# Gating values by a seven-product scheme, with u computed first

## The chip, the cores and the metric

The kernel runs on one core of a Trainium2 chip. The metric is the device time of one execution in microseconds (us). Five engines work side by side, each with its own instruction queue: TensorE (PE, matmuls), VectorE (DVE), ScalarE (ACT), GpSimd (POOL) and SyncE (SP, which here issues most of the loads). They wait for each other by semaphores.

## The reference, cut to what matters

One layer of a token mixer with 512 tokens of width 1024, and behind it a convolutional feed-forward. What is touched lies in the mixer:

```python
z = h @ w_in                       # (512, 1024) @ (1024, 7200)
u, vs, q, r, ga, gb, k, v, lr = _split(z, IN_SPLITS)
# spatial gating: 4 chunks of 128 tokens, 8 groups of 128 columns
vn = layer_norm(gelu(vs), ln_g, ln_b)
a  = gelu(u) * (einsum('gpq,bnqgc->bnpgc', w_s, vn) + b_s)
# bidirectional gated linear attention (GLA), 4 heads, chunks of 64 tokens
la = log_sigmoid(lr @ w2 + b2) / 16
o  = gla(q, k, v, la)              # products with exp(cumsum(la)), a state from chunk to chunk
ob = o * rsqrt(mean(o * o) + EPS) * g * silu(r)
merged = sigmoid(ga) * (a @ w_br_a) + sigmoid(gb) * (ob @ w_br_b)
return merged @ w_o
```

All of it is float32.

## The kernel before

Each float32 matmul is made of three: both operands are split into a high part (rounded to a short format) and a low part (the rest), and high x high, high x low and low x high are summed in PSUM. A product of 1024 x 1024 weights with all 512 tokens takes 192 matmuls of 128x512 in this way.

The weights come in tiles of 512 KB. A list, `specs`, sets their order. Each time the program asks for the next weights (`weights`), the loads further along in the list are issued on SP (`raw` tiles, five buffers) and the next tiles are split: ScalarE writes the high part `wh` (L152), VectorE the low part `wl` (L153). So the order of the list is also the order of this work on SP, ScalarE and VectorE.

Some products use a scheme of seven block products in place of eight (`w_strassen` L192 for the weights, `strassen` L474 for the matmuls): 7 x 24 = 168 matmuls. The weights' block sums are built partly by accumulating loads that POOL issues into `tt` tiles, partly by VectorE (L233, L245), the activations' sums `s1` to `s4` by `hx_sums` (L1281). Before the change the two output gates GA and GB, R, the output projection and the feed-forward's last matrix use it; the gating values vs, u, and the branches don't.

PSUM has eight banks, two pools of four: `mm` and `gl`. Accumulation, GLA's small products and transposes share them.

The stages around the change, in the program's order: the last GLA heads' work sits in a list `hooks`; `hook()` takes one step of it between groups of matmuls of the running stage. `steps(h)` (L1093) lists a head's steps: transposes, scores, state updates `step_u`, the next head's decays (`step_z`), and the outputs `step_o`. The decays of head 3 are computed on ScalarE as Abs, Exp, Ln for the log-sigmoid (L904, L915, L917 for the tokens, L872, L880, L881, L886 for the context) and Exp of the running sums (L935 to L937). VectorE multiplies the context's keys by the result (L952), and PE transposes the product (L970). Then:

1. vs: 192 matmuls (`wide_tm`), the remaining hooks beside them; Gelu and the statistics of the layer norm;
2. u: 192 matmuls, one block of 128 columns at a time, Gelu on ScalarE; beside it the normalisation of vs in 32 pieces of 128x128 (L1189) and the spatial gating, one group behind each block (`sgu_part`);
3. branch a: `a @ w_br_a`, first the left half in four `mm` banks, then the right half in four `gl` banks (`wide_kk`); beside it `hx_sums`;
4. GA, GB, R by the seven products, then branch b and the rest.

`tick` advances background work for later stages (VectorE's L1211) where it is called. ScalarE computes Exp, Ln, Gelu, Sigmoid and Sqrt from tables; where a function is not in the active table, the program has an instruction `ACT_TABLE_LOAD` ahead of it.

Of the kernel before, what the change touches and what calls it, by code (L numbers as in the profile page):

```python
# [33 lines left out]
def backbone_kernel(  # L34
# [157 lines left out]
    def w_strassen(w, c0, add_b12=False, low_first=False):  # L192
# [24 lines left out]
        def load_t(j):  # L217
            def load():
                tt[j] = [(late if low_first else heap)([P, 512], s="tt") for _ in range(2)]
# [76 lines left out]
    w_strassen(w_o[0], 0, True, True)  # L296
# [720 lines left out]
    def step_u(h, n0, n1):  # L1017
        S_ = heads[h]
        for n in range(n0, n1):
            for d in range(2):  # L1020
                i, j = (n, n + 1) if d == 0 else (3 - n, 2 - n)
                u = gl()
                mm3(u[:, :256], [z[:, i, :] for z in S_["kT"][d]], [z[:, i % 2, :] for z in S_["vx"][i // 2]],
                    True, True)
                raw = heap([P, 256], s="stt")
                V.tensor_tensor(raw, u[:, :256], S_["raw", d], op=ALU.add)
                V.tensor_scalar(raw, raw, S_["dec"][d][:, i:i + 1], None, op0=ALU.mult)
                S_["raw", d] = raw
                split_st(S_["st"][d][j], raw)

    def step_o(h, part):
        S_ = heads[h]
        for i in ((1, 2), (0, 3))[part]:
            po = gl()
# [132 lines left out]
    def vs_done(hf, t, ps):  # L1167
        vraw[hf][t] = late([P, 512], s="vr")
        A.activation(vraw[hf][t], ps, AF.Gelu)
# [16 lines left out]

    def vs_norm(g):
# [46 lines left out]
    crow = [late([110, P], s="crow") for _ in range(2)]  # L1234
    cw = ffn_conv_w[0].rearrange("a b (f p) -> (a b f) p", p=P)
    dma(crow[0], cw[0:110])
    dma(crow[1][0:88, :], cw[110:198])
    dma(crow[1][88:110, :], r8(ffn_conv_b[0]))
    ccol = const([P, 220], "ccol")

    def conv_cols(i):
        ps = gl()
        T.transpose(ps[:, :110], crow[i], ident[:110, :110])
        V.tensor_copy(ccol[:, i * 110:(i + 1) * 110], ps[:, :110])

# [4 lines left out]
    def sgu_part(j, ug):  # L1250
        ps = gl()
        for t in range(4):
            T.matmul(ps[:, t * P:(t + 1) * P], vsn[j][:, t, :], swT[j // 4][:, j % 4, :], start=True, stop=True)  # L1253
        s_ = heap([P, 4, P], s="sg")
        V.scalar_tensor_tensor(s_, ps.rearrange("p (t r) -> p t r", t=4), lng[:, j:j + 1],
                               sgb[j // 4][:, j % 4, :].unsqueeze(1).to_broadcast([P, 4, P]), op0=ALU.mult, op1=ALU.add)
        V.tensor_tensor(ug, s_.rearrange("p t r -> p (t r)"), ug, op=ALU.mult)
        a_act.append(split_act(ug, s="a", eng=A.copy))

    prev = None  # L1260
    vs_norm(0)
    for j in range(KT):
        w = weights()
        ps = mm()
        prod_cm(ps, w, hx)
        ug = heap([P, S], s="ug")
        A.activation(ug, ps, AF.Gelu)
        if prev is not None:
            sgu_part(*prev)
        prev = (j, ug)  # L1270
        if j in (3, 4):
            conv_cols(j - 3)
        if j < KT - 1:
            vs_norm(j + 1)
        tick(2 + j % 2)
    sgu_part(*prev)


    sums = {name: [] for name in ("s1", "s2", "s3", "s4")}

    def hx_sums():  # L1281

        a11, a21, a12, a22 = ([[z[:, c:c + 256] for z in hx[k0 + k]] for k in range(4)]
                              for k0, c in ((0, 0), (0, 256), (4, 0), (4, 256)))
        sums["a11"], sums["a12"], sums["a22"] = a11, a12, a22
        f_ = lambda z: z.bitcast(F32)
        s4_t = None
        for k in range(4):
            u, v = heap([P, 512], s="hu"), heap([P, 512], s="hv")
            s1, q, s3, s4 = u[:, :256], u[:, 256:], v[:, :256], v[:, 256:]  # L1290
            f1, f2 = heap([P, 512], s="hf"), heap([P, 512], s="hf")
            V.tensor_tensor(f1, f_(hx[k][0]), f_(hx[k][1]), op=ALU.add)
            V.tensor_tensor(f2, f_(hx[4 + k][0]), f_(hx[4 + k][1]), op=ALU.add)
            V.tensor_tensor(s1, f2[:, 256:], f1[:, 256:], op=ALU.subtract)
            V.tensor_tensor(s3, f1[:, :256], f1[:, 256:], op=ALU.subtract)  # L1295
            V.tensor_tensor(q, s1, f1[:, :256], op=ALU.add)
            V.tensor_tensor(s4, q, f2[:, :256], op=ALU.subtract)
            yield
            xh, xl = heap([P, 512], F32R, s="xh"), heap([P, 512], F32R, s="xl")
            if k % 2 == 0:  # L1300
                s4_t = heap([P, 512], F32R, s="s4h"), heap([P, 512], F32R, s="s4l")
            o = (k % 2) * 256
            h4, l4 = (z[:, o:o + 256] for z in s4_t)
            h3, l3 = a21[k]
            A.copy(h3, s3)
            V.tensor_tensor(l3, s3, f_(h3), op=ALU.subtract)
            A.copy(xh[:, :256], s1)
            A.mul(xh[:, 256:], q, -1.0)
            V.tensor_tensor(xl[:, :256], s1, f_(xh[:, :256]), op=ALU.subtract)
            V.scalar_tensor_tensor(xl[:, 256:], q, -1.0, f_(xh[:, 256:]), op0=ALU.mult, op1=ALU.subtract)  # L1310
            A.copy(h4, s4)
            V.tensor_tensor(l4, s4, f_(h4), op=ALU.subtract)
            sums["s1"].append((xh[:, :256], xl[:, :256]))
            sums["s2"].append((xh[:, 256:], xl[:, 256:]))
            sums["s3"].append((h3, l3))
            sums["s4"].append((h4, l4))
            yield
# [17 lines left out]

    def br_a_done(hf, t, ps):
        br[t][hf] = late([P, 512], s="br")
        A.copy(br[t][hf], ps)

    summing = hx_sums()  # L1340
    count = [0]

    def br_a_step():
        count[0] += 1
        if count[0] > KT:
            ada_bank[0] = mm
        if count[0] % 2:
            next(summing)
        else:
            tick(3 if count[0] <= KT else 4)  # L1350

    wide_kk(of_cols(a_act), br_a_done, br_a_step)
    a_act.clear()

    def ga_done(hf, t, src, sign):
        sg_ = src if sign < 0 and t > 1 else heap([P, 512], s="sga")
        A.activation(sg_, src, AF.Sigmoid, scale=sign)
        V.tensor_tensor(br[t][hf], br[t][hf], sg_, op=ALU.mult)

    of_sums = lambda name, k, t: [z[:, t * P:(t + 1) * P] for z in sums[name][k]]  # L1360
    ada_bank[0] = gl
    strassen(of_sums, ga_done, lambda: None)
# [32 lines left out]
    count[0] = 0  # L1395
# [562 lines left out]
```

## Time and profile before

| | us |
|---|---|
| median of 3 runs | 916.84 (916.72 to 916.93) |
| the profiled execution | 916.85 |
| its span in the profile | 914.9 |
| PE busy | 897.5 |
| DVE busy | 755.6 |
| ACT busy | 485.0 |
| POOL busy | 62.8 |

The profile is of one execution; times count from the span's start. Its mean granted TensorE clock is 0.996 of full speed. A row of the time line has the start, the time from the first start to the last end of what was merged, the engine, the line, the operation, output and inputs by the program's names, shape and count; in brackets the idle time before it and what ended that. Instructions that follow each other on one engine overlap a little in the records. Wait rows read: engine, line, what it waited for, us in all, times, longest.

### The profile page before, as it was taken

The page shows a single profiled execution, that of the slowest core. Times are in us where ns is not written, and L with a number is a line of the kernel's source. Part 1 is how long each engine was busy: PE and PEld are TensorE (multiplying, and loading weights), DVE is VectorE, ACT ScalarE, POOL GpSimd, SP SyncE. Part 2 cuts the span into 40 slices and gives each one's busy share as a digit, 9 for nine tenths or more (in the row PEclk, how much of TensorE's full clock was granted, in tenths as well). Part 3 has the DMA queues.
Part 4 walks back from the last instruction along what each step waited for, and adds up shares of the span by engine and source line. Part 5 has one row for each costly group of instructions (what it writes and reads, how often), then busy time and mean ns, then how long its engine had stood idle before and what let it go on. Part 6 is the DMA issues. An engine that isn't in the chain of part 4 may idle for free.

```text
span 914.9 us, 12857 instructions
## 1 busy us (share of the span) xinstructions
PE 897.5 (98%) x4671; PEld 755.7 (83%) x4671; DVE 755.6 (83%) x1308; ACT 485.0 (53%) x869; POOL 62.8 (7%) x98
## 2 busy tenths in 40 slices
PE   7999999999999999999999999999999999999996
PEld 5777899998888888888888879988888888888885
DVE  5667786889589878986776897899999888999796
ACT  5156554757366448575652569533333333467573
POOL 3000000000000011122011010000000000123000
PEclk9999999999999999999999999999999999999998
DMA  9960401045089385987586083263444333499522
GB/s 268 332 177 1 139 24 47 1 138 139 9 259 336 93 208 120 295 229 163 160 229 186 21 198 114 84 196 115 131 134 127 104 93 114 104 236 255 129 70 92
DMA packets 125820, 134.26 MB, mean 147 GB/s; under 512 B 7177, under 2 KB 84309, under 8 KB 125757
## 3 DMA queue, kind: packets, MB, share of 16 engines
q1 hardware_dynamic: 115357, 116.80, 41.4%
q0 software_dynamic: 8672, 15.43, 10.1%
q10 hardware_dynamic: 1728, 1.22, 0.4%
q8 instruction: 37, 0.61, 0.3%
q14 instruction: 26, 0.21, 0.1%
HBM read 131.32 MB, written 2.10 MB: 146 GB/s over the span
## 4 chain that ended last, share of the span: by engine, by line
PE 96%; DVE 2%; ACT 1%; DMA 0%; issue 0%; ACTq 0%
PE mm L406 32%; PE mm L437 11%; PE gl L484 9%; PE mm L484 7%; PE gl L1741 6%; PE mm L1741 4%; PE mm L430 4%; PE gl L437 4%; PE gl L956 3%; PE mm L421 3%; PE mm L729 2%; PE gl L729 1%; PE gl L652 1%; PE gl L989 1%; PE gl L1253 1%; PE mm L629 1%
## 5 line engine op out<-in xcount | busy, mean ns | idle before, releaser
L152 ACT CAST wh<-raw 128x1024 fp32r<-128x1024 f32 x110 | 114.7, 1049 | 102.5 <-PE mm L406 71.0
L153 DVE TENSOR_TENSOR wl<-raw,wh 128x1024 fp32r<-128x1024 f32 x110 | 133.4, 1219 | 27.0 <-ACT wh L152 21.8
L1624 DVE SCALAR_TENSOR_TENSOR cacc<-ca,ccol,cacc 128x441 f32<-128x441 f32 (+2 forms) x176 | 120.8, 692 | 6.1 <-ACT cacc L1612 2.8
L406 PE MATMUL mm<-h2h,wh 128*128 128x512 f32 x320 | 124.5, 389 | 0.0
L406 PE MATMUL mm<-h2l,wh 128*128 128x512 f32 x320 | 124.5, 389 | 0.0
L406 PE MATMUL mm<-h2h,wl 128*128 128x512 f32 x320 | 124.5, 389 | 0.0
L406 PEld LDWEIGHTS mm<-h2h,wl 128*128 128x128 f32 x320 | 60.1, 188 | 12.6
L406 PEld LDWEIGHTS mm<-h2l,wh 128*128 128x128 f32 x320 | 60.1, 188 | 12.5
L406 PEld LDWEIGHTS mm<-h2h,wh 128*128 128x128 f32 x320 | 60.1, 188 | 12.3
L1211 DVE SCALAR_TENSOR_TENSOR acc<-wa,c_col,acc 128x512 f32<-128x512 f32 x64 | 45.6, 745 | 4.0 <-DMA wa<-in_w_ada_dram 4.0
L1627 ACT ACTIVATE cacc<-cacc 128x512 f32<-128x512 f32 x22 | 13.9, 632 | 59.0 <-DVE cacc L1624 59.0
L406 PE MATMUL mm<-hxh,wh 128*128 128x512 f32 x104 | 41.7, 401 | 0.0
L406 PE MATMUL mm<-hxh,wl 128*128 128x512 f32 x104 | 41.1, 395 | 0.3 <-DVE wl L153 0.3
L406 PE MATMUL mm<-hxl,wh 128*128 128x512 f32 x104 | 40.6, 390 | 0.0
L232 ACT CAST wh<-tt 128x512 fp32r<-128x512 f32 x48 | 28.4, 619 | 17.9 <-PE mm L484 4.4
L233 DVE TENSOR_TENSOR wl<-tt,wh 128x512 fp32r<-128x512 f32 x48 | 31.6, 685 | 6.7 <-ACT wh L232 6.7
L208 POOL DMA_DIRECT2D tt<-in_w_in_dram x24 | 20.8, 1034 | 164.1 <-DVE hv L1295 72.3
L1683 ACT CAST wh<-raw 128x1024 fp32r<-128x1024 f32 x22 | 23.1, 1053 | 15.6 <-PE mm L1741 4.4
L1684 DVE TENSOR_TENSOR wl<-raw,wh 128x1024 fp32r<-128x1024 f32 x22 | 26.8, 1219 | 4.5 <-ACT wh L1683 4.3
L484 PE MATMUL mm<-wh,hxh 128*128 128x512 f32 x72 | 28.0, 389 | 0.0
L484 PE MATMUL mm<-wl,hxh 128*128 128x512 f32 x72 | 28.0, 389 | 0.0
L484 PE MATMUL mm<-wh,hxl 128*128 128x512 f32 x72 | 28.0, 389 | 0.0
(528 smaller groups left out, 2426.4 us busy)
## 6 DMA issues: line engine op xcount, KB each, us to landing
raw<-in_w_in_dram SPq DMA_DIRECT2D x54, 512.0 KB
wa<-in_w_ada_dram SPq DMA_DIRECT2D x96, 256.0 KB
raw<-in_ffn_w_up_dram SPq DMA_DIRECT2D x44, 512.0 KB
raw<-in_ffn_w_down_dram SPq DMA_DIRECT2D x22, 512.0 KB
tt<-in_w_in_dram POOLq DMA_DIRECT2D x24, 256.0 KB, 6.4
raw<-in_w_br_a_dram SPq DMA_DIRECT2D x8, 512.0 KB
raw<-in_w_br_b_dram SPq DMA_DIRECT2D x8, 512.0 KB
raw<-in_w_o_dram SPq DMA_DIRECT2D x8, 512.0 KB
```

What stands on the lines that cost most here:

```text
L152: A.copy(wh, raw)
L153: low = lambda: V.tensor_tensor(wl, raw, wh.bitcast(F32), op=ALU.subtract)
L232: A.copy(wh[:, kk, :], tt[j][kk])
L233: V.tensor_tensor(wl[:, kk, :], tt[j][kk], wh[:, kk, :].bitcast(F32), op=ALU.subtract)
L406: T.matmul(ps, a[:, k, :], b[:, c0:c0 + n], start=(k == 0 and i == 0), stop=(k == KT - 1 and i == 2))
L421: T.matmul(pss[u], a[:, k, :], b[:, c0:c0 + n], start=(k == 0 and z == 0), stop=(k == KT - 1 and z == 2))
L430: T.matmul(ps, a[:, t * P:(t + 1) * P], b[:, k % 4, :], start=(k == 0 and i == 0), stop=(k == KT - 1 and i == 2))
L437: T.matmul(ps, a, b[:, k % 2, :], start=(k == 0 and i == 0), stop=(k == KT - 1 and i == 2))
L484: T.matmul(ps[t], a, b[:, kk, :], start=(first and i == 0), stop=(j == 1 and kk == 1 and i == 2), skip_group_check=again)
L1211: V.scalar_tensor_tensor(a_, w_, c_col[:, k:k + 1], a_, op0=ALU.mult, op1=ALU.add)
L1624: V.scalar_tensor_tensor(o, a_[:, r0 + dy:r1 + dy, c0 + dx:c1 + dx], wcol(tap), o, op0=ALU.mult, op1=ALU.add)
L1741: T.matmul(ps, a[:, t * P:(t + 1) * P], w[b][:, j, c0:c0 + n], start=(first and i == 0), stop=(last and i == 2), skip_group_check=again)
```

## The change

1. The list of weights now has u ahead of vs, vs by the seven-product scheme, then GA, then branch a.
2. u comes first, with the remaining hooks beside it (head 2's last outputs, head 3's decays and all of head 3), the loads and transposes for the spatial gating's weights, and `hx_sums`. Its Gelus stand directly behind each block. The first three blocks take `mm` banks, the others `gl` banks. Head 3's state and output products use `mm` banks in place of `gl`.
3. vs by the seven products; beside it the spatial gating's bias and two transposes for the convolution's weights.
4. vs is normalised in place by 8 operations of 128x512. `sgu_part` runs under GA's products and works in PSUM in place; the result is split under GA's last steps and in branch a.
5. `ga_done` writes the sigmoid; branch a multiplies it by its own result on VectorE (before: a copy by ScalarE in branch a, and a multiplication in GA).
6. Branch a uses all eight banks, both halves together (`wide_all`), two ticks a step; GB has a tick at each step.

Lines of the changed kernel behind the first hunk stand 8 further down (L904 is L912, L970 is L978).

```diff
-    for hf in range(2):
-        for k in range(KT // 2):
-            w_cols(wi, O_VS + hf * 512, 512, 2 * k, 2)
     for j in range(KT):
         w_cols(wi, O_U + j * P)
-    w_wide(w_br_a[0])
+    w_strassen(wi, O_VS, True, pool=late)
     w_strassen(wi, O_GA)
+    for k in range(KT // 2):
+        for hf in range(2):
+            w_cols(w_br_a[0], hf * 512, 512, 2 * k, 2)
     w_strassen(wi, O_GB)
...
+    def wide_all(acts, done, step):
+        pss = [[pool() for _ in range(4)] for pool in (mm, gl)]
+        for k2 in range(KT // 2):
+            ws = [weights(2, 5) for _ in range(2)]
+            for kk in range(2):
+                for hf in range(2):
+                    for t in range(4):
+                        wide_step(pss[hf][t], ws[hf], acts, t, 2 * k2 + kk)
+                        if k2 == KT // 2 - 1 and kk:
+                            done(hf, t, pss[hf][t])
+                    step()
...
-                u = gl()
+                u = (gl if h + 1 < NH else mm)()
...
+    def u_slot():
+        slots[0] += 1
+        n = slots[0]
+        hook()
+        if n == 8:
+            sgu_load()
+        if n > 8:
+            next(summing)
+        if n in (11, 13):
+            sgu_turn((n - 11) // 2)
+
+    ug = []
+    for j in range(KT):
+        w = weights()
+        ps = (mm if j < 3 else gl)()
+        for k in range(KT):
+            prod_k(ps, w, hx, k, 0, S)
+            if k == 3:
+                u_slot()
+        ug.append(heap([P, S], s="ug"))
+        A.activation(ug[j], ps, AF.Gelu)
+        u_slot()
+    for low in s3_low:
+        low()
...
-    def vs_done(hf, t, ps):
+    def vs_done(hf, t, src, sign):
         vraw[hf][t] = late([P, 512], s="vr")
-        A.activation(vraw[hf][t], ps, AF.Gelu)
+        A.activation(vraw[hf][t], src, AF.Gelu, scale=sign)
         V.bn_stats(stats[:, t, hf, :], vraw[hf][t])
 
-    wide_tm(of_cols(hx), vs_done, hook)
-    while hooks:
-        hook()
...
+    strassen(of_sums, vs_done, vs_step)
...
-            A.activation(vsn[g][:, t, :], vraw[g // 4][t][:, (g % 4) * P:(g % 4 + 1) * P], AF.Identity,
-                         bias=vnb[:, t:t + 1], scale=vrs[:, t:t + 1])
+            A.activation(vraw[hf][t], vraw[hf][t], AF.Identity, bias=vnb[:, t:t + 1], scale=vrs[:, t:t + 1])
...
+    def ga_done(hf, t, src, sign):
+        br[t][hf] = late([P, 512], s="br")
+        A.activation(br[t][hf], src, AF.Sigmoid, scale=sign)
+
+    def ga_step():
+        slots[0] += 1
+        n = slots[0] - 5
+        if 0 <= n < KT:
+            sgu_part(n)
+        if n >= KT:
+            a_split()
+
+    strassen(of_sums, ga_done, ga_step)
...
+    def br_a_done(hf, t, ps):
+        V.tensor_tensor(br[t][hf], ps, br[t][hf], op=ALU.mult)
```

**Head 3's decays on ScalarE.** `lx` are the tokens' log decays (one tile a direction), `lm` the context's, `dec` the decays from chunk to chunk. Before, from the first Exp:

```order
L915 ACTIVATE lx_2412<-lx_2412 128x512
L915 ACTIVATE lx_2416<-lx_2416 128x512
L917 ACTIVATE lx_2412<-lx_2412,one_t 128x512
L917 ACTIVATE lx_2416<-lx_2416,one_t 128x512
L880 ACTIVATE lm_2423<-lm_2423 128x512
L152 CAST wh_2606<-raw_2473 128x1024
L935 ACTIVATE dec_2436<-dec_2436 128x4
L936 ACTIVATE mx_2414<-lx_2412 128x512
L881 ACTIVATE lm_2423<-lm_2423,one_t 128x512
```

And now (the same operations are L923, L925, L888, L943, L944; `ug` is u's Gelu):

```order
L923 ACT_TABLE_LOAD
L923 ACTIVATE lx_2393<-lx_2393 128x512
L923 ACTIVATE lx_2397<-lx_2397 128x512
L925 ACT_TABLE_LOAD
L925 ACTIVATE lx_2393<-lx_2393,one_t 128x512
L925 ACTIVATE lx_2397<-lx_2397,one_t 128x512
L888 ACT_TABLE_LOAD
L888 ACTIVATE lm_2404<-lm_2404 128x512
L1249 ACT_TABLE_LOAD
L1249 ACTIVATE ug_2481<-mm_2456 128x512
L943 ACT_TABLE_LOAD
L943 ACTIVATE dec_2417<-dec_2417 128x4
```

The Gelu of u's second block stands between Exp and the decays, and there are table loads where there was none.

The end of the same chain on ScalarE now (`junk` are sums of squares of head 2's outputs):

```order
L889 ACT_TABLE_LOAD
L889 ACTIVATE lm_2404<-lm_2404,one_t 128x512
L1050 ACTIVATE junk_2494,oss<-gl_2483 128x256
L1050 ACTIVATE junk_2507,oss<-gl_2496 128x256
L1050 ACTIVATE junk_2539,oss<-gl_2528 128x256
L894 ACT_TABLE_LOAD
L894 ACTIVATE lm_2404<-lm_2404 128x255 x2
L1050 ACTIVATE junk_2552,oss<-gl_2541 128x256
L1249 ACT_TABLE_LOAD
L1249 ACTIVATE ug_2566<-mm_2515 128x512
```

Ln of the context's decays, which stood beside the decays' exponentials, comes behind them, and three of the sums of squares stand between it and the last Exp.

**Head 3's transposes on PE**, where PE takes the end of that chain (`lm`), in u's third and fourth block (`mm_2515`, `gl_2599`):

```order
L406 MATMUL mm_2515<-hxl_723,wh_2450 128x512
L406 MATMUL mm_2515<-hxh_722,wl_2451 128x512
L978 MATMUL gl_2568<-ident,lm_2404 128x128 x4
L986 MATMUL gl_2577<-ident,lx_2393 128x128 x3
L986 MATMUL gl_2585<-ident,lx_2397 128x128 x3
L406 MATMUL gl_2599<-hxh_420,wh_2509 128x512
```

They stood between two groups of the gating values' matmuls; now u's third block is ahead of them and its fourth behind.

More of the change, by code (lines that the diff above doesn't have):

```diff
@@ L218, in load @@
             def load():
-                tt[j] = [(late if low_first else heap)([P, 512], s="tt") for _ in range(2)]
+                tt[j] = [pool([P, 512], s="tt") for _ in range(2)]
                 start = len(traced())
@@ L295, in backbone_kernel @@
     w_wide(w_br_b[0], scaled=True)
-    w_strassen(w_o[0], 0, True, True)
+    w_strassen(w_o[0], 0, True, True, late)
     for f in range(FT):
@@ L1033, in step_o @@
         for i in ((1, 2), (0, 3))[part]:
-            po = gl()
+            po = (gl if h + 1 < NH else mm)()
             oc = po[:, :256]
@@ new lines, in backbone_kernel, with sgu_load @@
+    sw, swT, sgb, crow = [], [], [], []
+    cw = ffn_conv_w[0].rearrange("a b (f p) -> (a b f) p", p=P)
+    ccol = const([P, 220], "ccol")
+    def sgu_load():
+        for i in range(2):
+            sw.append(late([P, 4, P], s="sw"))
+            dma(sw[i], sgu_w[0, 4 * i:4 * i + 4].rearrange("g p q -> p g q"))
+        for i in range(2):
+            sgb.append(late([P, 4, P], s="sgb"))
+            dma(sgb[i], sgu_b[0:1, 4 * i:4 * i + 4, :].rearrange("o g p -> o (g p)").to_broadcast([P, 512]))
+        crow.extend(late([110, P], s="crow") for _ in range(2))
+        dma(crow[0], cw[0:110])
+        dma(crow[1][0:88, :], cw[110:198])
+        dma(crow[1][88:110, :], r8(ffn_conv_b[0]))
@@ L1232, in ada2 @@
             yield
[L1234 to L1244, printed above, removed]
     bg.extend([ada2(("g1", "sh")), ada2(("sc",))])
@@ L1248, in backbone_kernel, with sgu_part @@
     a_act = []
-    def sgu_part(j, ug):
-        ps = gl()
+    def sgu_part(j):
+        ps = mm()
         for t in range(4):
[L1253 to L1317, printed above, removed]
@@ L1319, in backbone_kernel @@
-    br = [[None] * 2 for _ in range(4)]
+            T.matmul(ps[:, t * P:(t + 1) * P], vraw[j // 4][t][:, (j % 4) * P:(j % 4 + 1) * P],
+                     swT[j // 4][:, j % 4, :], start=True, stop=True)
+        V.scalar_tensor_tensor(ps.rearrange("p (t r) -> p t r", t=4), ps.rearrange("p (t r) -> p t r", t=4),
+                               lng[:, j:j + 1], sgb[j // 4][:, j % 4, :].unsqueeze(1).to_broadcast([P, 4, P]),
+                               op0=ALU.mult, op1=ALU.add)
+        V.tensor_tensor(ug[j], ps, ug[j], op=ALU.mult)
@@ L1320, in backbone_kernel, with br_a_step @@
+    def br_a_done(hf, t, ps):
+        V.tensor_tensor(br[t][hf], ps, br[t][hf], op=ALU.mult)
+    def br_a_step():
+        slots[0] += 1
+        if slots[0] % 2 and len(a_act) < KT:
+            a_split()
+        tick(2)
+    wide_all(lambda k, t: [z[:, t * P:(t + 1) * P] for z in a_act[k]], br_a_done, br_a_step)
+    a_act.clear()
+    ug.clear()
+    ada_bank[0] = mm
     todo = []
@@ L1334, in do @@
                 todo.pop(0)()
[L1336 to L1362, printed above, removed]
     gb = [[None] * 2 for _ in range(4)]
@@ L1393, in r_done @@
         todo.append(turn(sr, ob, (t, hf), mm if hf == 0 and t < 2 or hf and t > 1 else gl))
-    count[0] = 0
+    count = [0]
     def r_step():
```

81 lines of the change are left out of this document (65 added, 16 removed).

## The prediction

> **What bounds the kernel now.** I read the page first, then TensorE's waits, then the stages around the change, then the chain that ended last, piece by piece.
>
> ```profile
> PE 897.5 (98%) x4671; PEld 755.7 (83%) x4671; DVE 755.6 (83%) x1308; ACT 485.0 (53%) x869; POOL 62.8 (7%) x98
> PE 96%; DVE 2%; ACT 1%; DMA 0%; issue 0%; ACTq 0%
> PE mm L534 <- DMA rows<-in_b_ada_dram: 5.9, 1, 5.9
> PE mm L484 <- DVE wl L153: 0.6, 1, 0.6
> ```
>
> TensorE works for 897.5 of 914.9 us and makes 96% of the chain. Apart from 5.9 us at the start, its longest wait is 0.6 us. A matmul taken away is therefore time saved, and a wait put in is time lost.
>
> The six stages that are touched, from the first gating matmul to the end of R (columns: window; length; busy time of PE, weight loads, DVE, ACT, POOL; granted clock, DMA share, GB/s):
>
> ```profile
> 188.87:251.60 62.73, 62.73 (x352) 54.69 (x351) 48.38 (x108) 36.11 (x78) 2.11 (x6) 1.00 0.37 104
> 251.60:304.53 52.93, 52.93 (x264) 44.10 (x263) 47.49 (x76) 32.23 (x59) 0.00 (x0) 1.00 0.81 267
> 304.53:349.92 45.39, 45.39 (x202) 37.55 (x201) 38.91 (x71) 21.46 (x40) 4.50 (x6) 1.00 0.54 140
> 349.92:388.00 38.08, 38.08 (x169) 31.54 (x169) 31.80 (x44) 28.41 (x49) 6.87 (x8) 1.00 0.89 249
> 388.00:426.08 38.08, 38.08 (x169) 31.54 (x169) 30.12 (x40) 24.86 (x39) 6.95 (x8) 1.00 0.75 194
> 426.08:466.00 39.92, 39.92 (x186) 33.08 (x186) 31.13 (x45) 24.76 (x39) 3.49 (x4) 1.00 0.63 173
> ```
>
> PE never pauses in these 277 us. VectorE is idle for 14.4, 5.4, 6.5, 6.3, 8.0 and 8.8 us, 49.3 in all.
>
> **The change, part by part.** *Fewer matmuls.* The gating values need 192 matmuls of 128x512 now and 168 by seven products of 24. The chain shows the pace of such products:
>
> ```profile
> 349.92 10.88 PE mm L484 x48
> ```
>
> That is 10.88 / 48 = 0.2267 us each, so 24 fewer are worth 24 x 0.2267 = 5.44 us. The instruction orders show all other PE work in the same number and shape, so nothing else is saved there.
>
> *u first.* What stood beside the gating values, head 3's decays above all, now stands beside u, and u's Gelus come between the decays' operations. These are the rows of ScalarE for head 3's decays, then the one place where it passes from other work to Gelu, and the consumers of the chain on VectorE and PE:
>
> ```profile
> 199.07 0.70 ACT L998 CAST st<-stt 128x256 fp32r<-128x256 f32 x2
> 199.67 0.69 ACT L904 ACTIVATE lx<-gl,vec_b 128x512 f32<-128x512 f32 x1
> 200.26 0.47 ACT L872 ACTIVATE lm<-gl,vec_b 128x256 f32<-128x256 f32 x1
> 200.61 1.16 ACT L915 ACTIVATE lx<-lx 128x512 f32<-128x512 f32 x2
> 201.65 1.33 ACT L917 ACTIVATE lx<-lx,one_t 128x512 f32<-128x512 f32 x2
> 202.88 0.63 ACT L880 ACTIVATE lm<-lm 128x512 f32<-128x512 f32 x1
> 204.93 0.21 ACT L935 ACTIVATE dec<-dec 128x4 f32<-128x4 f32 x1 [0.49 <-DVE dec L930]
> 205.04 0.62 ACT L936 ACTIVATE mx<-lx 128x512 f32<-128x512 f32 x1
> 205.56 0.71 ACT L881 ACTIVATE lm<-lm,one_t 128x512 f32<-128x512 f32 x1
> 208.48 0.40 ACT L886 ACTIVATE lm<-lm 128x255 f32<-128x255 f32 x1
> 208.79 0.36 ACT L1042 ACTIVATE junk<-gl 128x256 bf16<-128x256 f32 x1
> ...
> 222.76 0.46 ACT L1013 ACTIVATE stt<-gl,dec 128x256 f32<-128x256 f32 x1
> 223.24 1.28 ACT L1169 ACT_TABLE_LOAD   x1
> 224.53 0.60 ACT L1169 ACTIVATE vr<-mm 128x512 f32<-128x512 f32 x1
> ...
> 210.48 0.68 DVE L952 TENSOR_TENSOR lm<-lm,kc 128x512 f32<-128x512 f32 x1
> ...
> 196.40 0.63 PE L899 MATMUL gl<-lrx,w2s 96*128 96x512 f32 x2
> 212.41 0.60 PE L970 MATMUL gl<-ident,lm 128*128 128x128 f32 x4
> ```
>
> Before, not one table load falls into this chain; Exp and Ln come from the set loaded at the start. In the changed order there are nine from u0's Gelu to u2's, seven of them on the chain (ahead of Exp, Ln, Exp, u1's Gelu, Exp, Ln, Exp). A load takes 1.28 us, starts when the operation before it is over (222.76 + 0.46 = 223.22, load at 223.24), and the next starts when it ends, so the overlap of about 0.1 us that neighbours have here is lost too. I take the same distance to the chain's start as before, since PE's work between L899 and L970 is the same (16.0 us). Both state casts now stand ahead of the four Abs, which end at about 201.0 rather than 200.73. Then:
> - loads: 7 x 1.28 = 9.0 us;
> - work: two Exp 1.16, two Ln 1.33, Exp 0.63, Gelu 0.60, the decays and their exponentials (0.11 + 0.52 twice, 0.52, 0.62) 2.4, Ln 0.61, three sums of squares 3 x 0.36 + 0.1, two Exp 0.71: together 8.6 us;
> - end of the last Exp 201.0 + 9.0 + 8.6 = 218.6, VectorE's product 0.68 and two hand-overs of about 0.05: 219.4.
>
> PE comes to these transposes at 212.4. It stands still for 219.4 - 212.4 = 7.0 us, with u's later matmuls queued behind. VectorE's scans and score factors run under the loads, and its own splits for the fifth u block, queued behind the late product, follow some 4 us after it, ahead of PE, which has 24 matmuls (5.4 us) of the fourth block in between. So nothing more comes of the same wait. Bounds: 6 us if the hand-overs and sums of squares cost nothing, 7.6 if every operation shows its whole duration.
>
> The Trainium skill ("ScalarE: Activation LUTs", What ACT_TABLE_LOAD costs) gives 1283 ns for the load and about 1380 ns more for a drain, some 2.66 us a switch. The trace agrees with the first figure (1.28) and shows no second one: 0.02 us before the load, 0.01 behind it. By the page the stall would be some 9.7 us longer.
>
> *The clock after such a stall.* No row shows PE idle for long between two stretches of work. The nearest are the end and the start of the program (the second fence is PE's warm-up line L629, its count of matmuls in each 2 us):
>
> ```profile
> 903.00:906.00 3.00, 2.89 (x20) 2.70 (x18) 1.91 (x7) 1.08 (x4) 0.00 (x0) 1.00 0.04 15
> 906.00:909.00 3.00, 0.00 (x0) 0.00 (x0) 2.50 (x9) 2.48 (x8) 0.00 (x0) 0.89 0.17 61
> 909.00:912.00 3.00, 0.00 (x0) 0.00 (x0) 1.51 (x4) 1.63 (x3) 0.00 (x0) 0.50 0.79 295
> ```
> ```profile
> 6.00:8.00 2.00, 1.95 (x5) 1.65 (x6) 1.00 1.10 305
> 8.00:10.00 2.00, 2.00 (x7) 1.56 (x6) 1.00 0.91 285
> 10.00:12.00 2.00, 2.00 (x9) 1.76 (x8) 1.00 1.13 308
> ```
>
> PE ends at 905.9; a mean of 0.89 between 906 and 909 is 0.5 for the last 0.66 us, so the clock halves 2.4 us after the last matmul. A stall of 7 us is longer. If full clock comes back as late as it went, 2.4 us at half speed cost 1.2 us. The start says much the same: 12 matmuls in 3.95 us where the later pace (9 in 2 us) gives 12 in 2.67, 1.3 us lost; but the granted clock reads 1.00 there. Ends: 0 and twice that, 2.6; I take 1.2. The Trainium skill ("TensorE: Matmul & The Clock Gate", Part 1) says half rate after an idle window of 3.4 us until a busy one of that length has passed; the halving at the end agrees, the return no row shows. By it the term would be 1.7 us.
>
> *Split and sums for the product scheme.* By the two orders VectorE gets 24 more operations of 128x512 and 8 fewer of 128x256:
>
> ```profile
> L233 DVE TENSOR_TENSOR wl<-tt,wh 128x512 fp32r<-128x512 f32 x48 | 31.6, 685 | 6.7 <-ACT wh L232 6.7
> L1040 DVE COPY o<-gl 128x256 f32<-128x256 f32 x16 | 6.2, 410 | 0.4 <-PE gl L956 0.4
> raw<-in_w_in_dram SPq DMA_DIRECT2D x54, 512.0 KB
> tt<-in_w_in_dram POOLq DMA_DIRECT2D x24, 256.0 KB, 6.4
> ```
>
> 24 x 0.685 - 8 x 0.41 = 13.2 us, in stages with 49.3 us idle: nothing, unless it bunches (a rival below). POOL issues 10 more accumulating loads (8 of 256 KB, 2 of 512 KB, 3 MB) with 6.4 us to land. By the order the last of the first set are issued as u's seventh block ends and are wanted 9.4 us later, the second product's start, so they have 3 us to spare and I cost them at 0; what they lack, PE would wait. SP's loads for spatial gating join its queue where the DMA share was 0.37 to 0.81: 0 too.
>
> *Spatial gating under GA.* Eight normalisations of 128x512 replace 32 of 128x128, and must be over before GA's third product takes its second bank, 12.2 us after GA starts (54 matmuls). The rows for Sqrt before:
>
> ```profile
> 252.75 1.28 ACT L1181 ACT_TABLE_LOAD   x1
> 257.07 0.31 ACT L1181 ACTIVATE var<-var,eps_t 128x20 f32<-128x20 f32 x1 [3.04 <-DVE var L1180]
> ```
>
> Last Gelu at 0.7, casts to 2.2, load 3.5, Sqrt 3.9, a bank's copy and a cast to 5.2, eight normalisations at about 0.53 (a 128x512 row less overlap) 9.4, the copy 10.0 to 10.6. It fits by 1.6 us: 0. Branch a's sigmoid first and product after, its eight banks, and the ticks moved to branch a and GB change no PE work; they lie under VectorE's idle time: 0.
>
> **Sum**, against the profiled execution of 916.85 us (span 914.9; the runs' median is 916.84): 916.85 - 5.44 + 7.0 + 1.2 = 919.6.
>
> **The rivals.**
> - *Clock unharmed*: the stall is as priced, but no half speed follows, as the start's granted clock of 1.00 suggests. 918.4.
> - *The loads hide* (the other side): ScalarE fetches a table while the operation before it still runs. If each load hid behind 0.6 us of work, the stall would be 7.0 - 7 x 0.6 = 2.8, near the 2.4 us of the clock, and the time 914.2; with no stall at all 911.4. It decides below 3.6 us of stall. The row at 223.24, which starts just behind its predecessor, speaks against it.
> - *More waits behind*: VectorE bunches where the new products begin, or the normalisations miss GA's bank. u and branch a leave it 5.4 and 6.5 us, half of the 13.2 could fall on each; two or three waits of 1 to 2 us give 921.5 to 925. For it: the margin of 1.6 us at GA; against it: PE's stall gives VectorE, the loads and SP 7 us to get ahead before the new products start.
> - *A switch drains*: before each load ScalarE empties for as long again as the load takes. 7 x 1.28 = 9.0 us more, 928.6. The rows at 223.24 and 224.53 speak against it. The Trainium skill's drain, in the section named above, is this rival.
>
> **How the numbers follow.** A change under 0.2% (1.8 us) can't be told from none. As forecast (918.7 to 921.5) 0.40; clock unharmed 0.20; more waits 0.22; loads hide 0.15; a drain 0.03. The time is the first's. Faster takes most of the hidden loads, 0.15; same the better part of the unharmed clock and a little of the rest, 0.22; slower what remains, 0.63. The range leaves out the drain, the stall-free end and the upper tail of the waits: 914 to 924.5; the likeliest alone has 918.7 to 921.5.
>
> **What would show it.** After: 15 table loads, nine around head 3's decays; one PE wait of 6 to 7.6 us at L978 on VectorE's L960, some 24 us into u; granted clock 0.5 around its end; 168 matmuls for the gating values at 0.227; no other PE wait over 1 us up to R's end. It is wrong if the wait at L978 is under 4 us, if the clock stays and other waits come, or if waits over 1 us stand at GA's third product or where the new products begin.

## The result, and the profile after

The changed kernel takes 933.25 us (median of 4 runs, 932.59 to 934.42) against 916.78 (916.68 to 916.93) before, in runs side by side: a ratio of 1.0181 [1.0163, 1.0199]. It is slower, as forecast, but by 16.5 us and not by 2.8, and it lies outside the range. The profiled execution took 932.99 us, its span is 931.3 (before 914.9).

The page's busy times, and its chain that ended last, by engine:

```profile
PE 898.0 (96%) x4647; PEld 754.1 (81%) x4647; DVE 766.6 (82%) x1324; ACT 490.6 (53%) x858; POOL 72.0 (8%) x108
PE 78%; DVE 8%; DMA 6%; ACT 5%; issue 1%; SPq 0%; ACTq 0%; POOL 0%; DVEq 0%; POOLq 0%
```

PE has its 24 matmuls fewer (4671 to 4647) and yet is busy 0.5 us longer; its share of the chain fell from 96% to 78%. The chain's piece with the gating values' products shows the same pace as before, 10.88 / 48 = 0.2267 us each:

```profile
260.83 10.88 PE mm L492 x48
```

PE's waits (us in all, times, longest):

```profile
PE gl L978 <- DVE lm L960: 7.1, 1, 7.1
PE mm L542 <- DMA rows<-in_b_ada_dram: 5.5, 1, 5.5
PE gl L492 <- ACT gl L501: 4.8, 1, 4.8
PE gl L1387 <- DVE sr L1424: 1.8, 1, 1.8
PE gl L1387 <- DVE sr L1426: 1.3, 1, 1.3
PE mm L1315 <- ACT es L506: 0.9, 1, 0.9
```

The second row is the start, as before. The first was forecast; the last four had no term in the sum.

**The stall in u.** ScalarE's time line through head 3's decays, and the PE row that waits for its end:

```profile
201.40 1.28 ACT L923 ACT_TABLE_LOAD   x1
...
217.16 1.28 ACT L894 ACT_TABLE_LOAD   x1
218.46 0.72 ACT L894 ACTIVATE lm<-lm 128x255 f32<-128x255 f32 x2
...
220.03 1.11 PE L978 MATMUL gl<-ident,lm 128*128 128x128 f32 x4 [7.13 <-DVE lm L960]
```

Seven loads of 1.28 us stand there, each followed by its operation 0.02 us or less behind it (217.16 + 1.28 = 218.44, then 218.46). The last Exp ends at 219.18; 218.6 was forecast. PE comes to its transposes half a microsecond late too, so the forecast 7.0 us and the measured 7.1 are nearer than their parts.

PE is out of work from 212.9 to 220.03. Windows of its clock (length; PE, weight loads, DVE, ACT, POOL; granted clock, DMA share, GB/s):

```profile
215.00:217.00 2.00, 0.00 (x0) 0.00 (x0) 0.92 (x2) 1.99 (x8) 0.10 (x1) 0.86 0.00 0
217.00:219.00 2.00, 0.00 (x0) 0.00 (x0) 0.36 (x1) 1.97 (x5) 0.10 (x1) 0.50 0.00 0
...
222.00:223.00 1.00, 1.00 (x4) 0.88 (x4) 1.00 (x2) 1.00 (x2) 0.00 (x0) 0.50 0.67 106
223.00:224.00 1.00, 1.00 (x5) 0.80 (x4) 0.83 (x2) 1.00 (x3) 0.00 (x0) 0.86 1.00 383
```

A mean of 0.86 in the first is half speed for its last 0.56 us: the clock halves at 216.4, 3.5 us after the last matmul, and by the last row it is back at 223.3, 3.3 us after PE resumed. PE's work in between took 5.58 us where the same operations at full speed take 3.83 (L978 0.44, L986 0.66, twelve matmuls 2.73): 1.75 us lost. Some 0.16 of it isn't the clock: the first product behind a wait lacks the overlap with the one before it (0.39 us each at a pace of 0.2267).

**The joint between the gating values and GA.** The window first, then, engine by engine, what leads to the normalisations:

```profile
298.33:312.30 13.97, 13.97 (x63) 11.50 (x63) 13.94 (x29) 7.99 (x14) 2.32 (x3) 1.00 0.20 44
```
```profile
301.07 0.60 ACT L1259 ACTIVATE vr<-gl 128x512 f32<-128x512 f32 x1 [0.32 <-PE gl L492]
...
308.93 1.28 ACT L1280 ACT_TABLE_LOAD   x1
310.33 0.31 ACT L1280 ACTIVATE var<-var,eps_t 128x20 f32<-128x20 f32 x1
...
311.82 5.75 ACT L1287 ACTIVATE vr<-vr,vnb,var 128x512 f32<-128x512 f32 x8 [0.15 <-DVE vnb L1284]
317.48 0.57 ACT L501 COPY gl<-mm 128x512 f32<-128x512 f32 x1
```
```profile
303.16 1.28 DVE L233 TENSOR_TENSOR wl<-tt,wh 128x512 fp32r<-128x512 f32 x2
...
305.10 1.29 DVE L233 TENSOR_TENSOR wl<-tt,wh 128x512 fp32r<-128x512 f32 x2
306.30 0.69 DVE L245 TENSOR_TENSOR tt<-tt,raw 128x512 f32<-128x512 f32 x1
306.91 0.69 DVE L1260 BATCH_NORM_STATS2 stats<-vr 128x6 f32<-128x512 f32 x1
...
308.10 0.69 DVE L1260 BATCH_NORM_STATS2 stats<-vr 128x6 f32<-128x512 f32 x1
```
```profile
318.10 0.80 PE L492 MATMUL gl<-wh,xh 128*128 128x512 f32 x1 [4.83 <-ACT gl L501]
```

VectorE is busy for 13.94 of 13.97 us. GA starts at 300.87 and the last Gelu ends at 301.67, but the statistics of that tile start at 308.10, 6.4 us later: they stand in VectorE's queue behind GA's splits (L233) and block sums (L245). So Sqrt comes 9.5 us after GA's start and not 3.9; eight normalisations take 5.75 us and not 4.2; the copy of the bank ends at 318.05, 17.2 us after the start and not 10.6; PE wants it at 12.4 (318.10 - 4.83 = 313.27). The clock halves here too:

```profile
314.00:316.00 2.00, 0.00 (x0) 0.00 (x0) 0.00 (x0) 2.00 (x4) 0.00 (x0) 0.86 0.87 167
316.00:318.00 2.00, 0.00 (x0) 0.00 (x0) 0.00 (x0) 2.00 (x5) 0.00 (x0) 0.50 1.12 203
...
320.00:322.00 2.00, 2.00 (x8) 1.71 (x7) 0.28 (x1) 2.00 (x3) 0.00 (x0) 0.50 0.29 45
322.00:324.00 2.00, 2.00 (x12) 1.77 (x12) 1.10 (x2) 0.83 (x1) 0.00 (x0) 0.93 0.61 225
```

It falls at 315.4, 2.2 us after the last matmul, and comes back at about 322.3, 4.2 us after PE resumed, which costs some 2.0 us.

**The end of R.** The same stretch in the kernel before and in the changed one, set by R's first product with the output gate (447.15 and 464.76):

```profile
438.79:467.69 28.90, 28.90 (x141) 24.06 (x141) 25.59 (x37) 18.41 (x30) 0.00 (x0) 1.00 0.53 165
```
```profile
456.40:485.30 28.90, 26.96 (x128) 21.46 (x126) 28.83 (x43) 20.69 (x35) 0.00 (x0) 1.00 0.62 204
```

VectorE has 43 operations there where it had 37, and no idle time left where it had 3.3 us. PE waits 3.1 us for its products.

**The sum of spans:** 931.3 - 914.9 = 16.4. Traced: -5.44 (matmuls) + 7.1 + 1.75 (stall in u and its clock) + 4.83 + 1.97 (GA and its clock) + 3.1 (R) + 0.9 = 14.2. The other 2.2 us don't lie in waits: PE is idle for 931.3 - 898.0 = 33.3 us against 17.4, and of these 15.9 more the five waits make 7.13 + 4.83 + 1.8 + 1.3 + 0.9 = 15.96, with 0.4 less at the start and about as much in small waits. They lie in PE's busy time, which with 24 matmuls fewer and the half clock should have fallen by 1.7 us and rose by 0.5. A part is the overlap that is lost at each wait; the rest I didn't trace.

### The profile page after: what moved, and what is told of

Read it like the earlier page. It is cut to its first block, busy times and chain, and to the rows that moved or that the text cites. A ratio compares the mean times of both kernels' runs of the same rounds, so it can differ in the third digit from the quotient of the medians.

```text
span 931.3 us, 12864 instructions
## 1 busy us (share of the span) xinstructions
PE 898.0 (96%) x4647; PEld 754.1 (81%) x4647; DVE 766.6 (82%) x1324; ACT 490.6 (53%) x858; POOL 72.0 (8%) x108
## 4 chain that ended last, share of the span: by engine, by line
PE 78%; DVE 8%; DMA 6%; ACT 5%; issue 1%; SPq 0%; ACTq 0%; POOL 0%; DVEq 0%; POOLq 0%
PE mm L406 27%; PE gl L492 8%; PE gl L1775 6%; PE mm L492 5%; PE mm L1775 4%; PE mm L437 4%; PE mm L430 4%; PE gl L406 4%; DMA wa<-in_w_ada_dram 3%; PE mm L421 2%; PE mm L737 2%; PE gl L964 2%; DMA tt<-in_w_in_dram 2%; PE gl L737 1%; DVE acc L1307 1%
## 5 line engine op out<-in xcount | busy, mean ns | idle before, releaser
L153 DVE TENSOR_TENSOR wl<-raw,wh 128x1024 fp32r<-128x1024 f32 x110 | 133.3, 1220 | 24.6 <-ACT wh L152 22.2
L232 ACT CAST wh<-tt 128x512 fp32r<-128x512 f32 x60 | 35.4, 620 | 34.8 <-DVE tt L245 15.9
L1307 DVE SCALAR_TENSOR_TENSOR acc<-wa,c_col,acc 128x512 f32<-128x512 f32 x64 | 45.4, 746 | 8.5 <-DMA wa<-in_w_ada_dram 8.3
L233 DVE TENSOR_TENSOR wl<-tt,wh 128x512 fp32r<-128x512 f32 x60 | 39.7, 684 | 5.9 <-ACT wh L232 5.8
L208 POOL DMA_DIRECT2D tt<-in_w_in_dram x32 | 27.5, 927 | 159.4 <-DMA tt<-in_w_in_dram 66.6
L492 PE MATMUL mm<-wh,hxh 128*128 128x512 f32 x96 | 38.0, 395 | 0.0
L492 PE MATMUL mm<-wh,hxl 128*128 128x512 f32 x96 | 37.4, 389 | 0.0
L492 PE MATMUL mm<-wl,hxh 128*128 128x512 f32 x96 | 37.4, 389 | 0.0
L492 PE MATMUL gl<-wh,xh 128*128 128x512 f32 x64 | 26.5, 415 | 5.0 <-ACT gl L501 4.8
L1697 POOL DMA_DIRECT2D b<-in_ffn_w_down_dram x11 | 10.1, 939 | 271.0 <-DMA b<-in_ffn_w_down_dram 257.4
L492 PE MATMUL gl<-wl,xh 128*128 128x512 f32 x64 | 25.5, 399 | 0.0
```

The source lines that it names most:

```text
L153: low = lambda: V.tensor_tensor(wl, raw, wh.bitcast(F32), op=ALU.subtract)
L232: A.copy(wh[:, kk, :], tt[j][kk])
L233: V.tensor_tensor(wl[:, kk, :], tt[j][kk], wh[:, kk, :].bitcast(F32), op=ALU.subtract)
L492: T.matmul(ps[t], a, b[:, kk, :], start=(first and i == 0), stop=(j == 1 and kk == 1 and i == 2), skip_group_check=again)
L1307: V.scalar_tensor_tensor(a_, w_, c_col[:, k:k + 1], a_, op0=ALU.mult, op1=ALU.add)
```

## The experiments

Theory: the order costs the stall in u (7.1 + 1.75 us), and VectorE, full at two joints, costs the rest. Rivals: ScalarE's own order at GA, the clock alone, late loads. Each ratio is against the kernel before on the same chip; its median was 917.00 for the first four, 917.04 for the next four, and 917.03 for the last three.

**1. Gelus behind the decays.** u's first three Gelus are held behind head 3's last decay on ScalarE (`z_last`); nothing else is changed.

```diff
-        A.activation(ug[j], ps, AF.Gelu)
+        u_ps.append(ps)
+        if j >= 2:
+            start = len(traced())
+            for i in range(3) if j == 2 else (j,):
+                A.activation(ug[i], u_ps[i], AF.Gelu)
+            behind(start, z_last[0])
```

> The changed kernel with one thing moved: the Gelus of u's first three blocks are held back until head 3's decays are done on ScalarE, so that the decays run with the table that is loaded from the start (7 table loads in all, the changed kernel has 15). Table loads are the cause of the wait at L978: no wait there and no half clock behind it, 7.1 + 1.8 us less: about 924.4; up to 3 us of it may come back further on, since VectorE, the loads and SP lose the time they had to get ahead. Rival, the wait comes from u being first at all (the decays' place beside u, or the late state casts): the wait at L978 stays above 4 us and the time above 930.

923.92 us (921.08 to 926.40), ratio 1.0063 [1.0043, 1.0083]: 9.3 us off the changed kernel's median. The profile is of the longest of the four runs. The wait at L978 is gone; R's two stand as they were (1.8 and 1.3), and most of GA's:

```profile
PE gl L492 <- ACT gl L501: 3.6, 1, 3.6
```

So Gelu between the decays cost 9.3 us here, near the 8.85 that the stall and its clock add up to, and the waits at the two joints don't depend on it. At GA the half speed lasted longer than before:

```profile
308.00:310.00 2.00, 0.09 (x1) 0.09 (x1) 0.00 (x0) 2.00 (x4) 0.00 (x0) 0.79 1.12 203
...
314.00:316.00 2.00, 2.00 (x8) 1.77 (x8) 0.91 (x2) 0.64 (x1) 0.00 (x0) 0.50 0.55 210
316.00:317.00 1.00, 1.00 (x6) 0.80 (x5) 1.00 (x2) 0.31 (x1) 0.00 (x0) 1.00 0.00 0
```

PE resumed at 309.92; the clock came back at 316.0, 6.1 us later.

**2. The bank's copy ahead of the normalisations.** On the changed kernel: the normalisations are issued in GA's steps, behind both copies that PE waited for.

```diff
-    for hf in range(2):
+    def vs_norm(hf):
...
         n = slots[0] - 5
+        if n in (-2, -1):
+            vs_norm(n + 2)
```

> The changed kernel with one thing moved: the eight normalisations of the gating values are issued in GA's third and fourth step, behind ScalarE's two copies of the first product into GA's second pair of banks, and not ahead of the second copy. The order on ScalarE is the cause of the 4.8 us wait for L501: that wait goes, with the 2.0 us of half clock behind it, and a wait of about 0.6 us for the first normalised tile comes in: about 927. Rival, VectorE's backlog decides (statistics and Sqrt come 5.6 us late whatever stands behind them): most of the wait moves to the first spatial-gating product (L1337) and the time stays above 930.

932.44 us (930.27 to 933.61), ratio 1.0163 [1.0147, 1.0179]. The wait for L501 is gone, and this one stands in its place:

```profile
PE mm L1337 <- ACT es L506: 4.5, 1, 4.5
```

PE's first product of the spatial gating reads the normalised tiles and a bank behind them; on ScalarE's time line of this run Sqrt is at 310.82 (in the changed kernel 310.33) and the last normalisations end at 319.27, the copies `es` behind them. Another order on ScalarE only moves the wait: the statistics are late, as the theory has it.

**3. The ticks out of GB, one more a step in branch a.** The second hunk is GB's step.

```diff
-        tick(2)
+        tick(3)
...
-        tick()
```

> The changed kernel with one thing moved: the 14 background steps beside GB (each a multiply-accumulate of 0.74 us on VectorE and a load of 256 KB) go to branch a, three steps a group there and none in GB. They are the cause of VectorE being late at R's end: the waits of 1.8 and 1.3 us before the last transposes (L1387) fall under 1 us together, and the time to about 930.5. Rival, VectorE is late because the accumulating loads for GB and R land late: the waits stay and the time stays at 933; or branch a is too full for 16 more steps, and waits of over 1 us come there.

932.25 us (931.39 to 933.46), ratio 1.0165 [1.0150, 1.0180]. R's waits fell from 3.1 to 1.4, not under 1 as expected, and the time can't be told from the changed kernel's (932.59 to 934.42). Inconclusive as to the time. In the stretch that was set by R's first product VectorE still has 43 operations and 28.75 us of work.

**4. The seven products undone, the order kept.** Gating values by 192 matmuls, behind u.

```diff
-    w_strassen(wi, O_VS, True, pool=late)
+    for hf in range(2):
+        for k in range(KT // 2):
+            w_cols(wi, O_VS + hf * 512, 512, 2 * k, 2)
...
-    strassen(of_sums, vs_done, vs_step)
+    wide_tm(of_cols(hx), lambda hf, t, ps: vs_done(hf, t, ps, 1.0), vs_step)
```

> The changed kernel with the seven-product scheme undone for the gating values alone (192 matmuls, u still first, all else as changed; the sums of the activations are still made beside u, and their s3 is split behind the gating values). 24 matmuls more: +5.4. If VectorE's splits and sums for that scheme make the statistics late, the wait for L501 at GA falls under 1 us with its half clock: 933.3 + 5.4 - 6.8 = about 932. If the order on ScalarE alone does it, the wait stays: about 938.7. The wait of 7.1 us at L978 stays in both.

933.45 us (933.37 to 933.67), ratio 1.0178 [1.0162, 1.0193]: with 24 matmuls more, as long as the changed kernel. The stall in u stays, GA has no wait left, and VectorE takes the last tile's statistics 0.1 us after its Gelu:

```profile
PE gl L980 <- DVE lm L962: 7.1, 1, 7.1
```
```profile
306.86 0.60 ACT L1258 ACTIVATE vr<-mm 128x512 f32<-128x512 f32 x1 [0.22 <-PE mm L439]
```
```profile
307.57 0.69 DVE L1259 BATCH_NORM_STATS2 stats<-vr 128x6 f32<-128x512 f32 x1
```

So the scheme itself makes GA's stall, and it gives its 5.44 us back there. It does two things at once: it gives VectorE more splits, and it finishes several output tiles together at its end, where this version spreads them. Which weighs more isn't separated.

**5. Seven table loads in the kernel before.** One-column Gelus among head 3's decays, each with a reload of the set of Exp and Ln.

```diff
+        A.activation(other[:, n:n + 1], src, AF.Gelu)
+        last = traced()[-1].name
+        start = len(traced())
+        A.preload_act_table_set("natural_log_exp_and_others")
+        behind(start, last)
```

> The kernel before, with table loads put into head 3's decays and nothing else changed: at three places a Gelu of one column, whose result nobody reads, and behind it the load of the set that was active. The order then has seven more loads, five of them ahead of the last Exp. By the same sum as in the prediction the last Exp ends at 215.5 and VectorE's product at 216.2, so PE, due at 212.4, waits 3.8 us; that is longer than the 2.4 us after which the clock halved at the end of the program, so some half clock follows (0.7 to 1.8 us): 921.3 to 922.5. If a stall did no harm to the clock: 920.6. If loads did not matter, and only what stands beside the decays did: 916.9.

920.43 us (920.05 to 921.00), ratio 1.0035 [1.0021, 1.0050]. PE's two new waits, and its clock beside each:

```profile
218.28 0.66 PE L992 MATMUL gl<-ident,lm 128*128 128x128 f32 x4 [1.11 <-DVE lm L974]
...
232.12 0.86 PE L978 MATMUL gl<-vx,kT 128*128 128x256 f32 x5 [1.68 <-DVE stt L1048]
```
```profile
216.00:218.00 2.00, 1.17 (x6) 0.63 (x4) 0.47 (x1) 1.97 (x3) 0.00 (x0) 1.00 0.00 0
...
230.00:232.00 2.00, 0.44 (x4) 0.23 (x2) 2.00 (x5) 1.99 (x4) 0.00 (x0) 1.00 1.21 288
```

This run differs from the kernel before in more than the loads. On PE 32 of the gating values' matmuls stand ahead of the transposes of `lm` (L992 here), where the kernel before has 12 (L970 there), so PE came to them at 217.2 and not at 212.4. And VectorE's product waited for a sixth load: the third one-column Gelu reads `lm`, and the product starts behind it, at 217.53. With PE's old order the wait would have been some 5.9 us (218.28 - 212.4, an estimate); with 20 matmuls more ahead of it, it was 1.1. The second wait is a state update 14 us later, with VectorE busy throughout. No half speed follows either. That the time is near the 920.6 of the rival is luck, since neither the wait of 3.8 us nor its place came true. The run shows that the loads delay PE without u first, and that work ahead of the joint hides most of the delay; load for load it can't be set against the 8.85 us.

**6. Both joints eased at GA.** Experiments 1 and 2 together, and the spatial gating two of GA's steps later.

```diff
-        n = slots[0] - 5
+        n = slots[0] - 7
+        if n in (-4, -3):
+            vs_norm(n + 4)
         if 0 <= n < KT:
             sgu_part(n)
-        if n >= KT:
+        if n >= KT - 2:
```

> The changed kernel with both joints eased: u's first three Gelus behind head 3's decays, the normalisations behind GA's two copies, and the spatial gating two steps (some 5.4 us) later under GA, so that VectorE's late statistics no longer hold up PE. If VectorE's backlog at the end of the gating values only delays the normalised tiles and nothing of PE's own products, no wait over 1 us is left before branch a, and the waits at R's end stay (3.1): 916.9 - 5.4 + 3.1 + 0.9 + about 2 in small pieces = 917.5. If the backlog delays GA's own splits too, waits of 2 to 4 us come at GA's third or fourth product: 920 to 922.

918.24 us (916.35 to 920.17, 10 runs), ratio 1.0012 [1.0003, 1.0021]. GA has no wait left; R's stands, and with it half speed:

```profile
PE gl L1397 <- DVE sr L1434: 2.0, 1, 2.0
```
```profile
464.00:466.00 2.00, 0.23 (x2) 0.23 (x3) 2.00 (x4) 2.00 (x5) 0.00 (x0) 1.00 0.85 272
466.00:468.00 2.00, 2.00 (x10) 1.73 (x9) 2.00 (x4) 1.46 (x3) 0.00 (x0) 0.60 0.80 240
468.00:470.00 2.00, 2.00 (x6) 1.51 (x6) 2.00 (x4) 0.09 (x1) 0.00 (x0) 0.54 1.03 349
```

The half speed runs from about 466.4 to 469.8, 3.4 us, and begins when PE has already resumed.

**7. The background loads three ahead.** Number 6, with the loads that VectorE's ticks wait for issued earlier.

```diff
+            while len(wa2) < min(i + 3, len(parts_)):
+                k_, _, c0 = parts_[len(wa2)]
+                wa2.append(late([P, 512], s="wa2"))
+                dma(wa2[-1], w_ada[0, k_ * P:(k_ + 1) * P, c0:c0 + 512])
```

> The same, and the loads of the background steps are issued three steps ahead of their use, with the same operations in the same order on VectorE. VectorE waited 7.8 us for these loads between 345 and 480 us in the changed kernel (2.1 in the kernel before). If that is why R's last transposes wait, the 3.1 us there fall under 1 us: about 915. If the backlog is of work and not of waiting, they stay: 917.5.

917.87 us (913.84 to 918.77, 10 runs), ratio 1.0003 [0.9993, 1.0014]. The median can't be told from number 6's, so earlier loads don't take R's waits away in most executions. The profiled execution is the one of 913.84, the other nine lie between 916.69 and 918.77; at R's end PE doesn't wait in it, though VectorE is busy for 28.57 of the same 28.90 us.

**8. The order alone.** Experiments 1 and 4 together: u first and spatial gating under GA, with 192 matmuls.

> The changed kernel without the seven-product scheme for the gating values and with u's first three Gelus behind head 3's decays: only the new order of the stages is left. The stall at L978 goes with its half clock (8.9): 933.45 - 8.9 = 924.6. What is left above the kernel before (916.9) is then the price of the order alone: the waits at R's end (3.1) and at GB's first background product (1.2), 0.5 at GA, and some 2.8 in small pieces. If the splits were the cause of R's waits too, they go here: about 921.5.

924.76 us (924.26 to 926.60), ratio 1.0086 [1.0071, 1.0101], 7.7 us above the kernel before without any of the scheme. With the scheme (number 1) the same order stands 6.9 us above it: of its 5.44 us, 0.8 show, less than the spread of the runs of either. The stall in u and its clock are worth 933.45 - 924.76 = 8.7 us here, much as in number 1. The profile, of the longest run, has no wait at GA; R's two stand (1.8 and 1.3), with 1.4 at the copy of a bank in R and 1.4 at GB's first background product. So GA's stall comes with the scheme, and R's waits come with the order and where it puts the ticks.

**9. Number 7 once more**, for a profile of another execution.

> The kernel with both joints eased and the background loads three steps ahead, once more: its times so far lie between 913.8 and 918.8 us, and the one that was profiled was the shortest and showed no wait of PE over 0.8 us after the start. If the others are longer by waits at R's end (transfers that land later in some executions), a profile of 917 to 918 us shows 2 to 4 us there, with VectorE waiting for background loads ahead of it. If they are longer elsewhere, it shows that place.

917.20 us, one run. PE waits at R's end again, and VectorE waits for the ticks' loads 3.7 us in all (1.9 in number 7's profile):

```profile
PE gl L1400 <- DVE sr L1439: 1.3, 1, 1.3
PE gl L1400 <- DVE sr L1437: 0.8, 1, 0.8
```

The same program waits in one execution and not in another. Loads that land later, with VectorE full, would explain it; two profiles don't show that they are the cause.

**10. Number 6 without ticks in GB's steps.**

```diff
-        tick()
```

> The kernel with both joints eased and no background steps beside GB; they run beside branch b instead, where 32 places for steps take the 28 that are left. No prefetch. If the steps beside GB (work and late loads in VectorE's queue) make R's last transposes wait, the 2.0 us there go and the time falls from 918.2 to about 916; if the accumulating loads for GB and R do, it stays at 918.

916.66 us (915.55 to 917.65, 10 runs), ratio 0.9997 [0.9988, 1.0006]. The stretch at R, set as in the two rows of the result:

```profile
434.68:463.58 28.90, 28.90 (x141) 24.04 (x140) 25.57 (x37) 18.38 (x30) 0.53 (x1) 1.00 0.49 165
```

VectorE's 37 operations and 25.57 us are the kernel before's again, and PE doesn't wait. So R's waits hang on those six operations more, where 3.3 us were free. Four of the changed kernel's 43 are the ticks' own, two multiply-accumulates (L1307) and two splits of the sums (L399); here none is left in the stretch.

**11. Number 10 with number 7's loads.**

> Both: the background loads three steps ahead, and none of the steps beside GB. No wait over 1 us is left up to R's end in most executions: 916.9 - 5.4 + about 2.5 in small waits (0.8 for kcT, 0.4 before branch a, the rest in pieces) = 914; at most 916. It would be faster than the kernel before by about 0.3%. If the time still lies at 918, the loss is not in the background steps.

916.46 us (915.70 to 918.15, 11 runs), ratio 0.9996 [0.9987, 1.0005]: no change that could be told from the kernel before, where 914 was expected. With the stalls gone, 5.44 us should have shown. The largest new waits:

```profile
PE mm L492 <- DVE wl L153: 1.0, 1, 1.0
PE gl L492 <- DVE wl L233: 0.8, 2, 0.4
PE gl L997 <- DVE kcT L759: 0.8, 1, 0.8
PE mm L492 <- ACT wh L232: 0.8, 1, 0.8
```

With one of 0.5 they come to 3.9 us, against 0.6 for the one such wait before; and PE is busy for 893.8 us where 897.5 - 5.44 = 892.1 was due, 1.7 more. 3.3 + 1.7 = 5.0 of the 5.44 are given back. Half of that lies at one place, the output projection, from the start of its first matmul to the start of its last, before and here:

```profile
515.56:555.00 39.44, 38.83 (x175) 31.67 (x173) 37.55 (x58) 27.77 (x47) 4.42 (x6) 1.00 0.58 148
```
```profile
512.70:554.61 41.91, 39.97 (x174) 31.42 (x173) 40.39 (x64) 28.07 (x46) 4.39 (x6) 1.00 0.56 141
```

It takes 2.5 us more here, and in number 10 (41.97); in the changed kernel and in numbers 6, 7 and 9 it takes 39.4 to 39.5. The waits for L153 and L233 above stand in it. VectorE has 64 operations there where it had 58, and the six more are the end of the ticks' work (L1334, L1338, L1518, L1519 of this run's kernel): pushed back, it came to stand in another stage where VectorE was nearly full. The other 2.5 us are in pieces of 0.8 us or less that I didn't trace to one cause, and no run eases the joints without the scheme, so what the scheme alone is worth stays open. The median of none of the versions lies clear below the kernel before; the single execution of 913.84 us in number 7, without a wait at R and with 39.44 us for the output projection, has a span of 912.1, 2.8 us below it.

## Why the prediction was wrong

- *Fewer matmuls, 5.44 us*: right (0.2267 us each, 24 fewer).
- *The stall in u, 7.0 us*: right, 7.1, with both of its ends half a microsecond later than forecast. The loads cost 1.28 each, and no drain or hiding showed, so both rivals on them fall. Experiment 1 took the stall away.
- *The clock, 1.2 us*: right in kind, 1.75 measured. The Trainium skill ("TensorE: Matmul & The Clock Gate", Part 1), with a window of 3.4 us each way, gave 1.7, and the trace agrees in u: it fell after 3.5 us and came back 3.3 us after PE resumed. At GA it does not, with 2.2 and 4.2 us, nor does the program's end, where the fall came after 2.4. The step that I had taken from the program's end, 2.4 us back as well as down, was too short.
- *"It fits by 1.6 us: 0"*: the step that failed most, 4.8 us and 2.0 of clock. Two terms in it: Sqrt at 3.9 us was 9.5, because I let VectorE's statistics follow the Gelu at once, and they stood 6.4 us in a queue of splits; and the normalisation at 0.53 was 0.72. I had taken a 128x512 row with a number for bias and scale, but this one reads both per partition; the eight single records are of 798 to 816 ns against 600 for Gelu. The Trainium skill ("ScalarE: Activation LUTs", What ACT_TABLE_LOAD costs) has about 280 ns + 0.833 ns an element with one such operand and some 93 for another, by estimate 800 for this form: the trace agrees.
- *VectorE's 13.2 us, "in stages with 49.3 us idle: nothing, unless it bunches"*: it bunched. The size was near (VectorE is busy 11.0 us longer in all), the hiding was wrong. The idle time of a stage says nothing about its joints: at GA's start VectorE was busy 13.94 of 13.97 us, and in the 37.50 us ahead of that (260.83 to 298.33) it was busy for 26.80. That is the rival *more waits behind*; its place at GA was named, but it was priced at 1 to 2 us a wait and given 0.22. The argument against it, that PE's stall lets VectorE get ahead, failed: the stall is 80 us ahead of the joint, and without it (experiment 1) GA's wait was 3.6 and not longer than 4.8.
- *The ticks, 0*: 3.1 us at R. They were moved into branch a and GB, whose windows showed 6 to 8 us of idle VectorE, but their last sums and splits came to stand in R, where 3.3 us were free (experiment 10).
- *POOL's and SP's loads, 0*: PE waits for none of them. VectorE's waits for the ticks' loads (7.8 us between 298 and 500) may be part of R's case: issuing them earlier (experiment 7) left the median where it was, and that they decide single executions (7 against 9) is not shown.

The terms that were priced well sum to -5.44 + 7.1 + 1.75 = 3.4 us; the ones set to nothing made 10.8 (4.83 + 1.97 + 3.1 + 0.9), and 2.2 in PE's busy time were not traced.

## What to carry to other kernels

Idle time of an engine, summed over a stage, hides added work only where it lies; take the busiest 10 to 15 us ahead of each joint, list what stands in that engine's queue in order, and follow the operation on which the next stage hangs through it. A saving on the bound engine shows only as far as its suppliers keep up at every joint: the shortest execution (913.84 us, experiment 7) kept 2.8 of the 5.44 us, and background work that was pushed out of one full joint cost 2.5 us at the next. Before putting a function with another table into a chain of Exp and Ln, count the loads that fall on the chain, and see whether PE has other work in the meantime: seven loads ahead of PE's transposes cost 8.85 us; in experiment 5, with 20 matmuls more ahead of them, loads cost 3.4.

## What the runs showed of the hardware

- After a long wait the half speed neither began nor ended after a fixed time. In stalls of 7.1, 4.8 and 3.6 us it began 3.5, 2.2 and 2.8 us after the last matmul and ended 3.3, 4.2 and 6.1 us after PE resumed. A wait of 2.0 us brought 3.4 us of half speed that began 0.6 us after PE had resumed, while waits of 1.8 and 1.3 us at the same place brought none. The four runs of experiment 1 differ with it: 926.40 us at a mean granted clock of 0.992, 921.08 at 0.997.
- Seven loads of ScalarE's tables in a row of dependent operations took 1.28 us each, with 0.02 us or less on either side.
